# First stage of a hybrid decoder layer: deeper W_in and key buffers, forget logits and token scaling on ScalarE, diagonal maxima in one pass

## The chip, the core and the metric

The kernel runs on one core of a Trainium2 chip. Five engines take part, each with an instruction queue of its own that it works off strictly in order: TensorE (PE in the profile; its weight loads are PEld), VectorE (DVE), ScalarE (ACT), GpSimd (POOL) and SyncE (SP, which here only issues DMAs). An instruction that waits for another engine, or for a DMA, holds back everything behind it on its own engine.

The metric is the device time of one execution in microseconds (us), as the median of several. The kernel before took 2691.55 us (three runs, 2686.87 to 2695.32).

## The reference, cut to what matters

One decoder layer over 2048 tokens of width 1024, all in float32. The change lies in the part before the softmax:

```python
a = rms_norm(h, pre_mix_g)                      # per token: h * rsqrt(mean(h^2)) * g
z = a @ w_in                                    # 1024 -> 2568 columns
q, k, v, f, u_sg, v_sg = split(z)               # 512, 512, 512, 8, 512, 512
log_f = log_sigmoid(f + f_bias)                 # 8 heads
c = cumsum(log_f, over tokens)
logits = q k^T / 8 + c[t] - c[s]   (causal), softmax, times v
u = gelu(u_sg); v = layer_norm(gelu(v_sg), ln_g, ln_b)
y_sg = u * (tril(w_s) @ v + b_s)                # within chunks of 128 tokens
```

What follows (the projection, a feed-forward part and a gated embedding) is not touched.

## The kernel before

The first stage runs over four **blocks** of 512 tokens (`block`, `b` = 0 to 3). In each block TensorE multiplies the transposed, normalised tokens (`wide`, eight places of 128 input rows) with six **groups** of W_in columns (`GROUPS`): v_sg (344 columns), the rest of v_sg with a part of u (344), f with the rest of u (344), q, k and v (512 each). A group has four steps `n` (128 tokens each, or 128 columns for q and k); a step is 24 matmuls (8 rows of W_in by 3 products of high and low halves) into one of **two** PSUM places `pacc`, and ends with an evacuation in `dones`. A step can only begin when the evacuation of the step two before it is done. Steps are counted 0 to 23 through a block; the f and u group is steps 8 to 11, q is 12 to 15.

Each piece of W_in is loaded by SP to a raw place (`wraw`, L319), cast to its high half by ScalarE (L96) and subtracted to its low half by GpSimd (L100) into one of 12 places `wsp`.

Around the steps, `mine` and `hooks` place further work:

- `fu_done` (L357, L358): VectorE adds the forget bias to 8 columns (`zf`), then ScalarE takes the gelu of the others (`ug`). The two instructions read the same PSUM place.
- `layer_norm` of v (L110, L111, L413 to L417): root on GpSimd, then for each of 4 tiles two VectorE operations (gain, bias), a GpSimd copy and a VectorE subtraction (`vn`).
- `x_norm` of the next block's tokens (L290 to L296): squares on ScalarE, sum on VectorE, the root (`xr`, L111) on GpSimd, and the scaling of each 128x1024 tile on VectorE (L296).
- `log_sigmoid` (L376 to L393): a polynomial on 128x32 numbers, all on VectorE but for the sigmoid.
- `qk_done` and `put_v`: ScalarE writes the high half and VectorE the low half of a 128x512 tile to one of two places `stg`, which SP stores.
- `maxima(b)`, for the block before, spread between the matmuls by `Filler`: for each head q times 512 keys at a time into a place `pM`, and the row maximum on VectorE (L172; on the diagonal also L175 with the causal mask). Its keys and queries come in by DMAs that ScalarE issues (L159, L165), keys into two places `KM`.

Blocks 0 to 2 prepare the tokens of the next block, block 3 does not. Attention follows at about 560 us, with the last block's maxima spread in it, and the feed-forward part from about 1165 us on. The instructions are not issued in the order of the Python text: a list scheduler orders each engine's queue when the program is built.

Of the kernel before, what the change touches and what calls it, by code (L numbers as in the profile page):

```python
# [34 lines left out]
def trunk(ctx, tc, x, p, w_in, f_bias, sg_ln_g, sg_ln_b, sg_w, sg_b, att_out_g, sg_out_g,  # L35
# [36 lines left out]
    c0_all = const1.tile([P, NB, H], F32, name="c0_all")  # L72
    dmask_r = const1.tile([P, P], F32R, name="dmask")
# [4 lines left out]
    ident_r = const1.tile([P, P], F32R, name="ident_r")  # L78
    ve.tensor_copy(ident_r, ident)
# [54 lines left out]
    NKM = 2  # L134
# [4 lines left out]
    for t in QM:  # L139
        ve.memset(t[HD:HD + 2].bitcast(F32), 1.0)  # L140

    def maxima(b):

        def rows(h, mh):
            ps = place_m()
            pe.transpose(ps[:8, :P], mh.rearrange("p a b -> p (a b)").bitcast(F32), ident)
            mr = msm.tile([8, P], F32, name="mr", bufs=1)
            sc.copy(mr, ps[:8, :P])
            for l in range(2):
                sy.dma_start(qS[b, h, P + l].rearrange("(t i) -> t i", i=P), mr[4 * l:4 * l + 4])  # L150

        last = None
        ps = place_m()
        pe.matmul(ps[:, :H], ident[:, 0:1].broadcast_to([P, P]), c_all[:, 4 * b], start=True, stop=True)
        ve.tensor_copy(c0_all[:, b], ps[:, :H])
        n = 0
        for h in range(H):
            q = QM[h % 2]
            sc.dma_start(q[:HD].bitcast(F32), qS[b, h, :HD])  # L159
            mx = msm.tile([P, 4, 6], F32, name="mx")  # L160
            po.memset(mx, NEG)
            for c in range(b + 1):
                km = KM[n % NKM]
                n += 1
                sc.dma_start(km[:HD + 2].bitcast(F32), kS[c, h, HD:])  # L165
                for tt in range(4):
                    w = TB if c < b else P * (tt + 1)
                    ps = place_m()
                    pe.matmul(ps[:, :w], q[:, tt * P:(tt + 1) * P], km[:, :w], start=True, stop=True)  # L169
                    full = w if c < b else w - P  # L170
                    if full:
                        ve.tensor_reduce(mx[:, tt, c:c + 1], ps[:, :full], AX.X, ALU.max)  # L172
# [48 lines left out]
    with ExitStack() as ph:  # L221
        cst = pool(ph, "cst1", 1)
        stg = pool(ph, "stg", 2)
        small = pool(ph, "small1", 2)
        wrp = pool(ph, "wrp", 3)
# [16 lines left out]
        ones = cst.tile([P, P], F32, name="ones")  # L242
# [4 lines left out]
        def prep_consts():  # L247
# [6 lines left out]
            ve.memset(ones, 1.0)  # L254
            po.affine_select(out=upper, in_=ones, pattern=[[1, P]], compare_op=ALU.is_ge, fill=0.0,
# [23 lines left out]
        def x_norm(st, parts, rest=None):  # L279
            ss = st["ss"]  # L280
            for t0, t1 in parts:
# [13 lines left out]
                for tt in range(t0, t1):  # L295
                    ve.tensor_scalar(st["xs"][tt], st["xs"][tt], r[:, tt - t0:tt - t0 + 1], None, ALU.mult)  # L296
# [31 lines left out]
        def block(b, aT, hooks, fill, first=None):  # L328
# [18 lines left out]
            def uv_done(tt, ps):  # L347
# [4 lines left out]
                ve.tensor_scalar(gv[:, tt], gv[:, tt], mu[:, tt:tt + 1], None, ALU.add)  # L352
                junk = sg1.tile([P, 512], F32, name="junk")
                sc.activation(junk, gv[:, tt], AF.Square, accum_out=ss[:, tt:tt + 1])

            def fu_done(tt, ps):
                ve.tensor_tensor(zf[:, tt], ps[:, :H], fb, ALU.add)  # L357
                sc.activation(ug[:, tt, :336], ps[:, H:344], AF.Gelu_apprx_tanh)  # L358
# [15 lines left out]
            def log_sigmoid():  # L374

                ve.tensor_scalar(e, zf, -1.0, None, ALU.mult)  # L376
                ve.tensor_tensor(e, zf, e, ALU.min)
# [31 lines left out]
            def layer_norm():  # L409

                r = rstd_of(small, ss, 4, AW, "lnr")
                for tt in range(4):
                    ve.scalar_tensor_tensor(gv[:, tt], gv[:, tt], r[:, tt:tt + 1], lng, ALU.mult, ALU.mult)  # L413
                    ve.tensor_tensor(gv[:, tt], gv[:, tt], lnb, ALU.add)
# [1222 lines left out]
```

## Time and profile before

| | us |
|---|---|
| median of three runs | 2691.55 (2686.87 to 2695.32) |
| the profiled execution's own time | 2682.36 |
| its span, first to last instruction | 2680.6 |

| engine | busy us | share of the span |
|---|---|---|
| PEld (weight loads) | 2123.4 | 79% |
| VectorE | 1843.5 | 69% |
| ScalarE | 1341.6 | 50% |
| GpSimd | 806.6 | 30% |

Most of the profile's groups name what ended the idle time of an engine ("<-ACT ug L358" reads: the engine stood until the ScalarE instruction of line 358 that writes `ug`). Matmuls overlap in the array, so the times of single matmuls add up to more than the time that passes; idle time of PE is what counts.

### The profile page before, as it was taken

The page shows a single profiled execution, that of the slowest core. Times are in us where ns is not written, and L with a number is a line of the kernel's source. Part 1 is how long each engine was busy: PE and PEld are TensorE (multiplying, and loading weights), DVE is VectorE, ACT ScalarE, POOL GpSimd, SP SyncE. Part 2 cuts the span into 40 slices and gives each one's busy share as a digit, 9 for nine tenths or more (in the row PEclk, how much of TensorE's full clock was granted, in tenths as well). Part 3 has the DMA queues.
Part 4 walks back from the last instruction along what each step waited for, and adds up shares of the span by engine and source line. Part 5 has one row for each costly group of instructions (what it writes and reads, how often), then busy time and mean ns, then how long its engine had stood idle before and what let it go on. Part 6 is the DMA issues. An engine that isn't in the chain of part 4 may idle for free.

```text
span 2680.6 us, 37427 instructions
## 1 busy us (share of the span) xinstructions
PE 2610.0 (97%) x12316; PEld 2123.4 (79%) x12316; DVE 1843.5 (69%) x3214; ACT 1341.6 (50%) x2632; POOL 806.6 (30%) x695
## 2 busy tenths in 40 slices
PE   8999999999999999989999999999999999999999
PEld 7797978777677777767787788888888888888887
DVE  5547586866877655588888677677786596875443
ACT  6443433358877777655555455445435544453111
POOL 5444343410000100244434223236360171401211
PEclk9999999999999999999999999999999999999999
DMA  5565756588977876455665854447466644673331
GB/s 168 149 186 142 204 143 170 139 219 213 230 190 189 182 180 148 128 173 202 207 200 178 305 178 148 148 148 272 152 196 218 197 155 131 215 246 112 110 120 61
DMA packets 440083, 472.62 MB, mean 176 GB/s; under 512 B 155088, under 2 KB 269520, under 8 KB 439888
## 3 DMA queue, kind: packets, MB, share of 16 engines
q1 hardware_dynamic: 429651, 454.16, 57.5%
q10 hardware_dynamic: 10237, 16.07, 2.2%
q8 instruction: 97, 1.59, 0.3%
q14 instruction: 98, 0.80, 0.1%
HBM read 336.28 MB, written 133.82 MB: 175 GB/s over the span
## 4 chain that ended last, share of the span: by engine, by line
PE 53%; DVE 2%; DMA 1%; issue 0%; POOL 0%; ACT 0%; SPq 0%; DVEq 0%; ACTq 0%
PE pf L106 17%; PE pf L105 17%; PE pf L104 17%; DMA w1raw<-in_w_ff_dram 1%; PE pf L1485 1%; DVE w1p L999 0%; DMA B<-jS 0%; DVE ws L1183 0%; PE pf L1023 0%; DVE C L999 0%; DVE hq L1202 0%; PE pf L1478 0%; DVE z L750 0%; DVE v L1242 0%; DVE B L999 0%
## 5 line engine op out<-in xcount | busy, mean ns | idle before, releaser
L104 PE MATMUL pf<-B,w1p 128*128 128x512 f32 x752 | 298.4, 397 | 5.0 <-ACT w1p L996 3.9
L106 PE MATMUL pf<-B,w1p 128*128 128x512 f32 x752 | 296.7, 395 | 5.2 <-DVE w1p L999 5.1
L105 PE MATMUL pf<-B,w1p 128*128 128x512 f32 x752 | 297.3, 395 | 0.0
L1210 POOL TENSOR_TENSOR hq<-hq,hq 128x512 f32<-128x512 f32 x128 | 197.4, 1552 | 327.8 <-ACT hq L1204 292.1
L660 DVE TENSOR_TENSOR hl<-pr,hl 128x512 fp32r<-128x512 f32 (+1 forms) x320 | 193.0, 612 | 101.7 <-ACT hl L659 88.4
L100 POOL TENSOR_TENSOR wsp<-wraw,wsp 128x344 fp32r<-128x344 f32 (+1 forms) x176 | 199.5, 1150 | 190.0 <-ACT wsp L96 177.1
L651 ACT ACTIVATE pr<-pS,bias 128x512 f32<-128x512 f32 (+1 forms) x320 | 196.3, 622 | 101.2 <-PE pS L647 65.5
L172 DVE TENSOR_REDUCE mx<-pM 128x1 f32<-128x512 f32 (+3 forms) x288 | 169.8, 597 | 72.9 <-PE pM L169 72.0
L104 PE MATMUL pacc<-wsp,wide 128*128 128x344 f32 (+1 forms) x480 | 166.7, 347 | 9.9 <-ACT ug L358 6.8
L104 PE MATMUL pf<-R,L 128*128 128x512 f32 x452 | 176.1, 390 | 0.0
L105 PE MATMUL pf<-R,L 128*128 128x512 f32 x452 | 176.1, 390 | 0.0
L106 PE MATMUL pf<-R,L 128*128 128x512 f32 x452 | 176.0, 389 | 0.0
L106 PEld LDWEIGHTS pf<-B,w1p 128*128 128x128 f32 x752 | 142.0, 189 | 40.2 <-DVE w1p L999 7.8
L104 PEld LDWEIGHTS pf<-B,w1p 128*128 128x128 f32 x752 | 141.6, 188 | 39.5 <-ACT w1p L996 4.6
L105 PEld LDWEIGHTS pf<-B,w1p 128*128 128x128 f32 x752 | 141.8, 189 | 31.4
L106 PE MATMUL pacc<-wsp,wide 128*128 128x344 f32 (+1 forms) x480 | 162.6, 339 | 0.6 <-DVE wide L117 0.6
L105 PE MATMUL pacc<-wsp,wide 128*128 128x344 f32 (+1 forms) x480 | 162.4, 338 | 0.0
L659 ACT CAST hl<-pr 128x512 fp32r<-128x512 f32 (+3 forms) x272 | 146.4, 549 | 6.7 <-PE pO L674 0.8
L999 DVE TENSOR_TENSOR L<-lr,L 128x512 fp32r<-128x512 f32 x113 | 98.8, 874 | 70.2 <-ACT L L996 69.8
L996 ACT CAST L<-lr 128x512 fp32r<-128x512 f32 x113 | 70.2, 621 | 152.2 <-PE pf L105 117.5
L999 DVE TENSOR_TENSOR w1p<-ws,w1p 128x512 fp32r<-128x512 f32 (+1 forms) x136 | 120.6, 890 | 30.0 <-ACT w1p L996 28.0
L996 ACT CAST w1p<-w1raw 128x512 fp32r<-128x512 f32 (+1 forms) x123 | 73.3, 598 | 127.2 <-PE pf L105 124.5
(446 smaller groups left out, 7191.7 us busy)
## 6 DMA issues: line engine op xcount, KB each, us to landing
hidC<-hq SPq DMA_DIRECT2D x224, 256.0 KB
lr<-hidC SPq DMA_DIRECT2D x224, 256.0 KB
w1raw<-in_w_ff_dram SPq DMA_DIRECT2D x64, 512.0 KB
w1raw<-in_w_ff_dram SPq DMA_DIRECT2D x128, 256.0 KB
wraw<-in_w_in_dram SPq DMA_DIRECT2D x96, 256.0 KB
wraw<-in_w_in_dram SPq DMA_DIRECT2D x88, 172.0 KB
KM<-kS ACTq DMA_DIRECT2D x80, 132.0 KB
jS<-C SPq DMA_DIRECT2D x19, 512.0 KB
```

The costliest lines, as they stand in the source:

```text
L100: e.tensor_tensor(dst[:, 1], src, dst[:, 0].bitcast(F32), ALU.subtract)
L104: pe.matmul(ps, l[0], r[0], start=first, stop=False)
L105: pe.matmul(ps, l[0], r[1], start=False, stop=False)
L106: pe.matmul(ps, l[1], r[0], start=False, stop=last)
L172: ve.tensor_reduce(mx[:, tt, c:c + 1], ps[:, :full], AX.X, ALU.max)
L651: sc.activation(pr[:, off:], ps[:, off:], AF.Exp, bias=bias_of(b)[:, j, h:h + 1])
L659: sc.copy(hl[:, 0, off:], pr[:, off:])
L660: ve.tensor_tensor(hl[:, 1, off:], pr[:, off:], hl[:, 0, off:].bitcast(F32), ALU.subtract)
L996: sc.copy(dst[:, 0], src)
L999: (po if lo == "pool" else ve).tensor_tensor(dst[:, 1], src, dst[:, 0].bitcast(F32), ALU.subtract)
L1210: po.tensor_tensor(t, x, y, op)
L1485: pe.transpose(ps[:, kk], hts[t][g][:, kk * P:(kk + 1) * P], ident)
```

## The change

In the first stage:

- six raw W_in places (`wrp`) for three, three evacuation places (`stg`) for two;
- four key places `KM` for two, and key loads issued two pieces ahead, query loads one head ahead;
- `fu_done` copies the forget logits with ScalarE, and the bias is added for four tiles at once in `log_sigmoid`;
- the scaling of tokens is cut into halves of 512 columns that ScalarE does (for the first two tiles of the kernel VectorE does one half);
- the mean of v is no longer subtracted in a pass of its own: ScalarE's square takes it as a bias, and the gain and bias passes of `layer_norm` become two fused operations;
- the polynomial uses fused operations, 10 in place of 17;
- the diagonal's maximum is one fused operation over the whole width with a 128x512 mask `wmask`, in place of a reduction and a masked operation of 128;
- the matrix of ones is gone; the triangle's last column stands in for it.

```diff
@@
+    ident_r = const1.tile([P, P], F32R, name="ident_r")
+    ve.tensor_copy(ident_r, ident)
...
-    NKM = 2
+    NKM, LEAD = 4, 2
...
+    wmask = mst.tile([P, TB], F32, name="wmask")
+    ve.memset(wmask[:, :TB - P], 0.0)
+    ve.tensor_copy(wmask[:, TB - P:], dmask)
...
+        def load_k(i):
+            h, c = divmod(i, b + 1)
+            if h < H:
+                sc.dma_start(KM[i % NKM][:HD + 2].bitcast(F32), kS[c, h, HD:])
...
-            sc.dma_start(q[:HD].bitcast(F32), qS[b, h, :HD])
...
+                load_k(n + LEAD)
+                if c == b:
+                    load_q(h + 1)
                 n += 1
-                sc.dma_start(km[:HD + 2].bitcast(F32), kS[c, h, HD:])
...
-                    full = w if c < b else w - P
-                    if full:
-                        ve.tensor_reduce(mx[:, tt, c:c + 1], ps[:, :full], AX.X, ALU.max)
-                    if c == b:
-                        dg = ps[:, w - P:w]
-                        ve.tensor_tensor_reduce(out=dg, in0=dg, in1=dmask, scale=1.0, scalar=NEG,
-                                                op0=ALU.add, op1=ALU.max, accum_out=mx[:, tt, 5:6])
+                    if c < b:
+                        ve.tensor_reduce(mx[:, tt, c:c + 1], ps, AX.X, ALU.max)
+                    else:
+                        ve.tensor_tensor_reduce(out=ps[:, :w], in0=ps[:, :w], in1=wmask[:, TB - w:], scale=1.0, scalar=NEG,
+                                                op0=ALU.add, op1=ALU.max, accum_out=mx[:, tt, c:c + 1])
...
-        stg = pool(ph, "stg", 2)
+        stg = pool(ph, "stg", 3)
-        wrp = pool(ph, "wrp", 3)
+        wrp = pool(ph, "wrp", 6)
...
-                    ve.tensor_scalar(st["xs"][tt], st["xs"][tt], r[:, tt - t0:tt - t0 + 1], None, ALU.mult)
+                    for hf in range(2):
+                        xh, rt = st["xs"][tt][:, hf * 512:(hf + 1) * 512], r[:, tt - t0:tt - t0 + 1]
+                        if rest is not None and not hf:
+                            ve.tensor_scalar(xh, xh, rt, None, ALU.mult)
+                        else:
+                            sc.activation(xh, xh, AF.Copy, scale=rt)
...
-                ve.tensor_scalar(gv[:, tt], gv[:, tt], mu[:, tt:tt + 1], None, ALU.add)
                 junk = sg1.tile([P, 512], F32, name="junk")
-                sc.activation(junk, gv[:, tt], AF.Square, accum_out=ss[:, tt:tt + 1])
+                sc.activation(junk, gv[:, tt], AF.Square, bias=mu[:, tt:tt + 1], accum_out=ss[:, tt:tt + 1])
 
             def fu_done(tt, ps):
-                ve.tensor_tensor(zf[:, tt], ps[:, :H], fb, ALU.add)
+                sc.copy(zf[:, tt], ps[:, :H])
                 sc.activation(ug[:, tt, :336], ps[:, H:344], AF.Gelu_apprx_tanh)
...
-                ve.tensor_scalar(e, zf, -1.0, None, ALU.mult)
-                ve.tensor_tensor(e, zf, e, ALU.min)
+                ve.tensor_tensor(zf, zf, fb.unsqueeze(1).broadcast_to([P, 4, H]), ALU.add)
+                ve.scalar_tensor_tensor(e, zf, -1.0, zf, ALU.mult, ALU.min)
...
-                for k in (13, 11, 9, 7, 5, 3, 1):
-                    ve.tensor_tensor(pl, pl, s2, ALU.mult)
-                    ve.tensor_scalar(pl, pl, 1.0 / k, None, ALU.add)
-                ve.scalar_tensor_tensor(pl, pl, -2.0, s_, ALU.mult, ALU.mult)
+                ve.tensor_scalar(pl, s2, 1.0 / 17, None, ALU.mult)
+                for k in (15, 13, 11, 9, 7, 5, 3):
+                    ve.scalar_tensor_tensor(pl, pl, 1.0 / k, s2, ALU.add, ALU.mult)
+                ve.scalar_tensor_tensor(pl, pl, 1.0, s_, ALU.add, ALU.mult)
...
-                    ve.scalar_tensor_tensor(gv[:, tt], gv[:, tt], r[:, tt:tt + 1], lng, ALU.mult, ALU.mult)
-                    ve.tensor_tensor(gv[:, tt], gv[:, tt], lnb, ALU.add)
+                    ve.scalar_tensor_tensor(gv[:, tt], gv[:, tt], mu[:, tt:tt + 1], lng, ALU.add, ALU.mult)
+                    ve.scalar_tensor_tensor(gv[:, tt], gv[:, tt], r[:, tt:tt + 1], lnb, ALU.mult, ALU.add)
```

The scheduler orders the queues anew. The first place is **ScalarE in block 0, around the gelus of steps 8 to 10** (`zf` forget logits, `ug` gelu, `xss` the squares of the next block's tokens, `xt<-xt,xr` their scaling, `wsp` casts of W_in). Before:

```order
L290 ACTIVATE junk,xss<-xt 128x512
L358 ACTIVATE ug<-pacc 128x336
L96 CAST wsp<-wraw 128x512
L290 ACTIVATE junk,xss<-xt 128x512 x4
L358 ACTIVATE ug<-pacc 128x336
L290 ACTIVATE junk,xss<-xt 128x512 x2
L96 CAST wsp<-wraw 128x512
L358 ACTIVATE ug<-pacc 128x336
```

and of the change (L376 is the copy of the logits, L377 the gelu, L305 the squares, L316 the scaling):

```order
L305 ACTIVATE junk,xss<-xt 128x512 x2
L376 COPY zf<-pacc 128x8
L377 ACTIVATE ug<-pacc 128x336
L305 ACTIVATE junk,xss<-xt 128x512 x5
L376 COPY zf<-pacc 128x8
L377 ACTIVATE ug<-pacc 128x336
L316 ACTIVATE xt<-xt,xr 128x512 x6
L376 COPY zf<-pacc 128x8
L377 ACTIVATE ug<-pacc 128x336
```

Six scalings of the next block's tokens now stand ahead of the third copy and gelu (step 10). In blocks 1 and 2 three stand there.

The second place is **VectorE in block 0 from the root of the layer norm on** (`lnr` the root's argument, `gv` the gelu of v, `vn` its halves, `xss` and `xr` the tokens' sums and the root's argument). Before:

```order
L110 TENSOR_SCALAR lnr<-lnss 128x4
L413 SCALAR_TENSOR_TENSOR gv<-gv,lnr,lng 128x512 x2
L357 TENSOR_TENSOR zf<-pacc,fb 128x8
L414 TENSOR_TENSOR gv<-gv,lnb 128x512 x2
L413 SCALAR_TENSOR_TENSOR gv<-gv,lnr,lng 128x512
L417 TENSOR_TENSOR vn<-gv,vn 128x512 x2
L414 TENSOR_TENSOR gv<-gv,lnb 128x512
L357 TENSOR_TENSOR zf<-pacc,fb 128x8
L413 SCALAR_TENSOR_TENSOR gv<-gv,lnr,lng 128x512
L417 TENSOR_TENSOR vn<-gv,vn 128x512
L414 TENSOR_TENSOR gv<-gv,lnb 128x512
L293 TENSOR_TENSOR xss<-xss 128x1 x3
```

and of the change:

```order
L110 TENSOR_SCALAR lnr<-lnss 128x4
L431 SCALAR_TENSOR_TENSOR gv<-gv,mu,lng 128x512
L432 SCALAR_TENSOR_TENSOR gv<-gv,lnr,lnb 128x512 x2
L435 TENSOR_TENSOR vn<-gv,vn 128x512
L432 SCALAR_TENSOR_TENSOR gv<-gv,lnr,lnb 128x512
L435 TENSOR_TENSOR vn<-gv,vn 128x512
L432 SCALAR_TENSOR_TENSOR gv<-gv,lnr,lnb 128x512
L435 TENSOR_TENSOR vn<-gv,vn 128x512
L308 TENSOR_TENSOR xss<-xss 128x1
L435 TENSOR_TENSOR vn<-gv,vn 128x512
L110 TENSOR_SCALAR xr<-xss 128x1
L308 TENSOR_TENSOR xss<-xss 128x1 x2
```

The forget logits are gone from this queue, and after the root each tile needs one operation on `gv` in place of two; the first root argument of the tokens (`xr`) stands behind all four subtractions.

The third place is **GpSimd in block 0 behind the root of the layer norm** (`lnr`). Before:

```order
L111 TENSOR_TENSOR lnr<-lnr,mhalf 128x4
L100 TENSOR_TENSOR wsp<-wraw,wsp 128x512 x2
L415 TENSOR_SCALAR vn<-gv 128x512 x2
L100 TENSOR_TENSOR wsp<-wraw,wsp 128x512
L415 TENSOR_SCALAR vn<-gv 128x512 x2
L111 TENSOR_TENSOR xr<-xr,mhalf 128x1 x2
```

and of the change:

```order
L111 TENSOR_TENSOR lnr<-lnr,mhalf 128x4
L100 TENSOR_TENSOR wsp<-wraw,wsp 128x512
L433 TENSOR_SCALAR vn<-gv 128x512 x4
L111 TENSOR_TENSOR xr<-xr,mhalf 128x1 x3
L100 TENSOR_TENSOR wsp<-wraw,wsp 128x512 x4
L111 TENSOR_TENSOR xr<-xr,mhalf 128x1
```

Three roots now follow each other, and the fourth stands behind four subtractions of W_in.

More of the change, by code (lines that the diff above doesn't have):

```diff
@@ L77, in trunk @@
                      base=0, channel_multiplier=1)
-    ident_r = const1.tile([P, P], F32R, name="ident_r")
-    ve.tensor_copy(ident_r, ident)
     def bcast(pool, name, v, n):
@@ L156, in maxima, with load_q @@
         n = 0
+        def load_k(i):
+            h, c = divmod(i, b + 1)
+            if h < H:
+                sc.dma_start(KM[i % NKM][:HD + 2].bitcast(F32), kS[c, h, HD:])
+        def load_q(h):
+            if h < H:
+                sc.dma_start(QM[h % 2][:HD].bitcast(F32), qS[b, h, :HD])
+        load_q(0)
+        for i in range(LEAD):
+            load_k(i)
         for h in range(H):
             q = QM[h % 2]
-            sc.dma_start(q[:HD].bitcast(F32), qS[b, h, :HD])
-            mx = msm.tile([P, 4, 6], F32, name="mx")
+            mx = msm.tile([P, 4, NB], F32, name="mx")
             po.memset(mx, NEG)
@@ L241, in trunk @@
         sgb = cst.tile([P, H], F32, name="sgb")
-        ones = cst.tile([P, P], F32, name="ones")
         upper = cst.tile([P, P], F32, name="upper")
@@ L253, in prep_consts @@
             ve.memset(csum[:, 0], 0.0)
-            ve.memset(ones, 1.0)
-            po.affine_select(out=upper, in_=ones, pattern=[[1, P]], compare_op=ALU.is_ge, fill=0.0,
+            ve.memset(upper, 1.0)
+            po.affine_select(out=upper, in_=upper, pattern=[[1, P]], compare_op=ALU.is_ge, fill=0.0,
                              base=0, channel_multiplier=-1)
@@ L382, in log_sigmoid @@
                 ve.tensor_tensor(s2, s_, s_, ALU.mult)
-                ve.tensor_scalar(pl, s2, 1.0 / 17, 1.0 / 15, ALU.mult, ALU.add)
-                for k in (13, 11, 9, 7, 5, 3, 1):
-                    ve.tensor_tensor(pl, pl, s2, ALU.mult)
-                    ve.tensor_scalar(pl, pl, 1.0 / k, None, ALU.add)
-                ve.scalar_tensor_tensor(pl, pl, -2.0, s_, ALU.mult, ALU.mult)
+                ve.tensor_scalar(pl, s2, 1.0 / 17, None, ALU.mult)
+                for k in (15, 13, 11, 9, 7, 5, 3):
+                    ve.scalar_tensor_tensor(pl, pl, 1.0 / k, s2, ALU.add, ALU.mult)
+                ve.scalar_tensor_tensor(pl, pl, 1.0, s_, ALU.add, ALU.mult)
                 ve.tensor_scalar(zf, zf, 0.0, None, ALU.min)
-                ve.tensor_tensor(pl, pl, zf, ALU.add)
+                ve.scalar_tensor_tensor(pl, pl, -2.0, zf, ALU.mult, ALU.add)
                 ve.tensor_copy(car[:, 0], csum[:, b])
@@ L397, in run_sum @@
                 pe.matmul(ps[:, :32], upper, pl.rearrange("p a h -> p (a h)"), start=True, stop=False)
-                pe.matmul(ps[:, :32], ones, car[:, 0:4].rearrange("p a h -> p (a h)"), start=False, stop=True)
+                pe.matmul(ps[:, :32], upper[:, P - 1:P].broadcast_to([P, P]), car[:, 0:4].rearrange("p a h -> p (a h)"), start=False, stop=True)
                 ve.tensor_copy(c_all[:, 4 * b:4 * b + 4].rearrange("p a h -> p (a h)"), ps[:, :32])
```

## The prediction

> **What bounds the kernel now.** I began with the table of stretches, one row for each part of the first stage in which TensorE stood, then the waits of TensorE over these stretches (25 to 560 us).
>
> ```profile
> core 0: us, PE busy (x) PEld busy (x) DVE busy (x) ACT busy (x) POOL busy (x), PEclk, DMA share, GB/s
> 0.00:25.00 25.00, 17.86 (x72) 14.01 (x72) 17.27 (x47) 17.25 (x45) 12.76 (x23) 0.80 0.79 223
> 25.00:74.00 49.00, 43.26 (x274) 42.10 (x272) 26.11 (x56) 28.41 (x82) 25.92 (x27) 0.99 0.41 123
> ...
> 178.00:240.00 62.00, 55.58 (x281) 47.74 (x280) 47.25 (x138) 28.00 (x73) 33.78 (x35) 0.94 0.48 128
> ...
> 330.00:370.00 40.00, 33.77 (x168) 27.04 (x167) 38.15 (x94) 17.75 (x43) 23.34 (x24) 1.00 0.47 127
> ...
> 460.00:560.00 100.00, 92.49 (x478) 77.70 (x477) 80.63 (x216) 36.85 (x85) 47.08 (x51) 1.00 0.54 152
> ```
>
> The stage is TensorE's: the change leaves its matmuls as they are, so only its idle time can go. Length less PE busy gives 5.74 us in block 0's stretch, 6.42 in block 1's, 6.23 in block 2's (where VectorE is busy 38.15 of 40 us) and 7.51 in block 3's. What it waited for (us in total, times, longest):
>
> ```profile
> PE pacc L104 <- ACT ug L358: 9.0, 5, 2.5
> PE pM L169 <- DVE mx L172: 4.8, 8, 1.3
> PE pacc L104 <- DVE stg L117: 4.3, 3, 1.9
> PE tp L440 <- DVE gv L435: 2.7, 2, 1.6
> PE pacc L106 <- POOL wsp L100: 1.5, 3, 0.9
> PE pmx L104 <- DVE gv L427: 1.3, 1, 1.3
> ```
>
> The first row names ScalarE's gelu. The tile `zf` tells whom ScalarE itself waited for (its columns are shortest, median and longest ns; then us and times of a wait):
>
> ```profile
> L357 DVE TENSOR_TENSOR zf<-pacc,fb x16: 150/152/156, 60.8 to 498.4; 128x8 f32<-128x8 f32 x16
> L377 DVE TENSOR_TENSOR lse<-zf,lse x4: 179/1262/1279, 77.9 to 502.3; 128x32 f32<-128x32 f32 x4
> ...
>   ACT ug L358: 34.3, 14
> ```
>
> VectorE's addition of 0.15 us held the gelu 34.3 us in 14 cases, since it is queued behind the layer norm. So the first row's five waits are VectorE's queue too, as the next three rows are by name. Three stretches of slower clock follow on such waits:
>
> ```profile
> 73.40:77.00 3.60, 3.60 (x9) 2.84 (x10) 2.90 (x7) 1.11 (x3) 3.38 (x4) 0.53 0.20 67
> ...
> 203.00:206.70 3.70, 3.70 (x14) 3.54 (x15) 3.69 (x12) 1.97 (x6) 1.04 (x2) 0.54 0.26 72
> ...
> 216.70:220.20 3.50, 3.05 (x7) 2.48 (x8) 3.33 (x9) 1.56 (x5) 2.60 (x3) 0.51 0.28 75
> ```
>
> At a clock near 0.53, each costs 3.6 x 0.47 = 1.7 us, 5.1 in all. The Trainium skill, "TensorE: Matmul & The Clock Gate", Part 1, has the half clock come after an idle window of about 3.4 us; here it came though no wait exceeded 2.5 us, so the trace speaks against that length. By the rule the shortening of such waits would return no clock, and my sum would be 1.7 us less.
>
> **Block 0.** The timeline of TensorE, with the wait in brackets:
>
> ```profile
> 61.46 0.43 PE L104 MATMUL pacc<-wsp,wide 128*128 128x344 f32 x1 [2.01 <-ACT ug L358]
> 67.07 0.43 PE L104 MATMUL pacc<-wsp,wide 128*128 128x344 f32 x1 [1.56 <-ACT ug L358]
> 73.29 0.69 PE L104 MATMUL pacc<-wide,wsp 128*128 128x512 f32 x1 [2.17 <-ACT ug L358]
> 88.11 0.50 PE L104 MATMUL pacc<-wide,wsp 128*128 128x512 f32 x1 [1.78 <-DVE stg L117]
> ```
>
> The first two waits go: the copy and the gelu need only ScalarE, with squares ahead of them. The third has a new cause: six token scalings stand ahead of the third gelu, and they need roots behind the whole layer norm. Durations for that chain:
>
> ```profile
> L413 DVE SCALAR_TENSOR_TENSOR gv<-gv,lnr,lng 128x512 f32<-128x512 f32 x16 | 21.0, 1315 | 4.5 <-POOL lnr L111 4.5
> ...
> L417 DVE TENSOR_TENSOR vn<-gv,vn 128x512 fp32r<-128x512 f32 x16 | 16.4, 1027 | 1.6 <-POOL vn L415 1.6
> ...
> L414 DVE TENSOR_TENSOR gv<-gv,lnb 128x512 f32<-128x512 f32 x16 | 13.2, 829 | 0.0
> ```
>
> ```profile
> L290 ACT ACTIVATE junk<-xt 128x512 f32<-128x512 f32 x24 | 15.1, 631 | 0.4
> ...
> L358 ACT ACTIVATE ug<-pacc 128x336 f32<-128x336 f32 x16 | 7.2, 451 | 37.5 <-DVE zf L357 34.3 <-PE pacc L106 3.2
> ...
> L148 ACT COPY mr<-pM 8x128 f32<-8x128 f32 x22 | 5.4, 246 | 19.0 <-PE pM L146 19.0
> ```
>
> ```profile
> L111 POOL TENSOR_TENSOR xr<-xr,mhalf 128x1 f32<-128x1 f32 x12 | 8.3, 697 | 5.7 <-DVE xr L110 3.9 <-DVE xss L293 0.9 <-PE pM L169 0.8
> ```
>
> ```profile
> 56.34 1.02 POOL L111 TENSOR_TENSOR lnr<-lnr,mhalf 128x4 f32<-128x4 f32 x1
> ```
>
> From the root's end at 57.36: four fused operations at 1.315 and four subtractions at 1.027 are 9.37 (the fourth mean-and-gain pass runs while the root is computed), 0.3 for the tiny sums: 67.0. One root of 0.697, then six scalings at the squares' 0.631 (the copy form isn't in the trace; a square is the same tile): 71.5; copy 0.246 and gelu 0.451: 72.2. TensorE wants this place at 73.29 less 2.17, 2.01 and 1.56, that is 67.55: a wait of 4.7. The lower end takes all eight at L414's 0.829, the cheapest two-input row of this size: 6.63, and a wait of 1.9. I take **3.5**, nearer the upper end, whose rows are of the same operations. The fourth wait, 1.78 us for the low half of q behind the polynomial, goes: seven of its 17 operations go, and the token scalings on VectorE ahead of them. So block 0 gains 5.74 + 1.78 - 3.5 = **4.0 us**.
>
> **Blocks 1 and 2** have the same chain, with three scalings in front and with maxima between:
>
> ```profile
> 191.79 1.02 POOL L111 TENSOR_TENSOR lnr<-lnr,mhalf 128x4 f32<-128x4 f32 x1
> ...
> 334.36 1.01 POOL L111 TENSOR_TENSOR lnr<-lnr,mhalf 128x4 f32<-128x4 f32 x1 [1.26 <-DVE lnr L110]
> ```
>
> ```profile
> L172 DVE TENSOR_REDUCE mx<-pM 128x1 f32<-128x512 f32 (+3 forms) x288 | 169.8, 597 | 72.9 <-PE pM L169 72.0
> ```
>
> ```profile
> 202.89 0.46 PE L104 MATMUL pacc<-wsp,wide 128*128 128x344 f32 x1 [2.52 <-ACT ug L358]
> ...
> 208.54 0.39 PE L104 MATMUL pacc<-wide,wsp 128*128 128x512 f32 x1
> ...
> 338.55 0.33 PE L169 MATMUL pM<-KM,QM 128*128 128x128 f32 x1 [0.82 <-DVE mx L172]
> ...
> 342.75 0.45 PE L169 MATMUL pM<-KM,QM 128*128 128x384 f32 x1 [1.34 <-DVE mx L172]
> ...
> 349.36 0.40 PE L104 MATMUL pacc<-wide,wsp 128*128 128x512 f32 x1
> ```
>
> Block 1: the root ends at 192.81; 9.4 of layer norm, 1.8 for three maxima at 0.597 or less, 0.4 of sums, one root (0.7), three scalings (1.9), copy and gelu (0.7): 207.7. It is wanted at 208.54 - 2.52 - 1.7 of clock = 204.3: a wait of up to 3.4, and 0.7 with L414's 0.829. I take **2.5**, and leave 0.9 for small waits on W_in: 6.42 - 3.4 + 1.7 for one of its two slow stretches = **4.7 us**. Block 2: the root ends at 335.37; four fused operations and three subtractions (8.3), six maxima (3.6), sums (0.3); then one subtraction and one maximum (1.6) ahead of the second root's argument, that root (0.7), the third scaling (0.6), copy and gelu (0.7): 351.2. It is wanted at 349.36 - 0.82 - 1.34 = 347.2: a wait of up to 4.0, and 1.3 with the shorter operations. I take **3.0**: 6.23 - 3.0 = **3.2 us**.
>
> **Block 3** scales no tokens. Its waits for the scaling of `gv` (L435, 2.7) stay as they are in the code; half of L427's 1.3 I leave too; those for maxima and polynomial go. 7.51 - 3.3 = **4.2 us**.
>
> **Costed at nothing.** Three more raw places and the new `stg`: W_in's lows kept TensorE 1.5 us in the whole stage, which I gave back above. Key loads ahead are hidden by matmuls now and later; ScalarE, on which they queue, is busy 28 to 58% in these stretches. The diagonal's one pass trades a fixed cost for none, beside matmuls. At the start VectorE gets three more fillings ahead of the first tokens:
>
> ```profile
> 1.13 1.03 DVE L138 MEMSET KM<- 128x512 f32 x2
> ```
>
> That is about 1.4 us later; half-width scaling returns some 0.9 of it. I take -0.5, between -1.5 and +2 (7.14 us are idle there and evacuations now stand ahead of squares). Attention: 0, from -1 to +1.
>
> **The sum:** 4.0 + 4.7 + 3.2 + 4.2 - 0.5 = 15.6, say 16 us. The profiled execution took 2682.36 (span 2680.6), so 2666.4 for one like it; the median of the runs shown is 9.2 us higher, 2691.55, and I forecast from it: **2675.5 us**.
>
> **Rivals.**
>
> 1. *The scaling wait stays small.* If the roots come early, the three waits (9.0) and the other two slow stretches (3.4) go as well: 16 + 12.4 = 28 us, 2663. The ceiling, all idle time of the four stretches (25.9), the 1.78 and the 5.1 of clock, is 33 us: 2659. For it: ScalarE had slack in each stretch. Against: the queue rows, three to six scalings ahead of a gelu.
> 2. *VectorE's chain is not shortened.* The `lse` row above shows one operation at 0.18 and at 1.26 us: where it meets a GpSimd subtraction it waits. The new chain has as many exposed operations as the old. Then the waits are 4.7, 3.4 and 4.0, 3.1 more than I took, the `stg` waits (4.3) stay, and so does the clock's 1.7: 16 - 9.1 = 7 us gained, 2684.5. The Trainium skill, "SBUF — State Buffer", Who interferes with whom, says that a VectorE instruction with two SBUF inputs contends with a GpSimd instruction that reads SBUF, the loser waiting for the whole instruction; the fused operations all have two, and the `lse` row agrees.
> 3. *Slower: ScalarE's queue is the new bound.* On GpSimd the tokens' roots compete with W_in's subtractions:
>
> ```profile
> L100 POOL TENSOR_TENSOR wsp<-wraw,wsp 128x344 fp32r<-128x344 f32 (+1 forms) x176 | 199.5, 1150 | 190.0 <-ACT wsp L96 177.1
> ```
>
> If the scaling ahead of the third gelu had to wait for a root behind four of them (4.6), with the root and the scaling (1.3) the wait before q grows from 4.7 to 10.6 us, in three blocks 32 against the 9 assumed: 2691.55 - 16 + 23 = 2698.5. It turns the sign from about 8 us per block on (25 in all). Against: only the fourth root stands behind four subtractions in block 0's rows.
> 4. *The change doesn't do what it says:* a deeper buffer that SP fills no earlier. It is not in the sum, so it would change nothing.
>
> **How the numbers follow.** Forecast (gain 8 to 26 us) 0.57; rival 1 0.13; rival 2, and any case that ends within 8 us of before, 0.23; rival 3 0.07. 0.3% is 8 us, about what a measurement of this kernel can tell from no change. Faster is 0.57 + 0.13 = 0.70, same 0.23, slower 0.07. The range runs from the ceiling, 2659, to 2691, no gain: beyond it lie rival 3 and the worse half of rival 2, under 2 in 10.
>
> **What would show it.** Right: no wait of a `pacc` matmul for the gelu in the first two cases of each block; the wait for `ug` before the first q step named by ScalarE scalings and 2 to 5 us long; no `stg` wait behind the polynomial; slow stretches of the clock two or fewer in blocks 0 and 1. Wrong: waits at the first q step of 8 us or more, or new waits for W_in's low halves, since GpSimd now does roots and copies in a row.

## The result, and the profile after

The changed kernel took 2670.56 us (median of 7, 2667.26 to 2682.38) against 2687.77 us for the kernel before (7 runs, 2685.51 to 2695.32) on the same chip: a ratio of 0.9933, 95% interval 0.9913 to 0.9953, or 18 us faster by the ratio (13 to 23), 17 by the medians.

The two profiled executions don't show it: both have a span of 2680.6 us. The changed kernel's was the slowest of its seven; the other's, at 2682.36, was faster than all seven of its own. So each was profiled once more. What came out is read best from one row per execution: the stretch from the start to the first matmul of attention (its end is the start of the first `pS` matmul). Columns: the stretch in us, its length, busy time (and count) of PE, PEld, DVE, ACT and POOL, the clock, and DMA share and GB/s. Before, in two executions:

```profile
0.00:564.76 564.76, 529.94 (x2763) 455.63 (x2763) 360.18 (x925) 244.43 (x570) 252.60 (x272) 0.98 0.60 165
```

```profile
0.00:570.80 570.80, 535.71 (x2763) 460.06 (x2763) 361.82 (x925) 244.66 (x570) 252.26 (x272) 0.97 0.59 164
```

After, in two executions:

```profile
0.00:553.30 553.30, 525.38 (x2761) 455.67 (x2761) 325.09 (x784) 263.63 (x617) 245.71 (x272) 0.98 0.61 169
```

```profile
0.00:549.42 549.42, 524.13 (x2760) 454.39 (x2761) 328.44 (x787) 263.85 (x617) 246.03 (x272) 0.99 0.61 170
```

The first stage ends at 567.8 us before and 551.4 after, as means of two: 16.4 us. Attention, first to last `pS` matmul, took 547.8 and 555.1 us before, 558.9 and 550.9 after, so it moves by 7 to 8 us from one execution to the next of either kernel; behind it lie 1566 to 1568 us in all four. The gain is the first stage's, and the profiled execution of after lost it again in attention by chance.

Length less PE busy is idle time; but PE busy itself fell too, for the same matmuls. The clock records of the trace say why in part: TensorE runs at 0.50 in stretches of 3.4 us, and half of the time that it was busy in them is lost. Split in three, as means of the two executions:

| first stage, us | before | after | gain |
|---|---|---|---|
| TensorE idle | 35.0 | 26.6 | 8.4 |
| lost to the half clock | 11.9 | 7.8 | 4.1 |
| the rest: busy at full clock | 520.9 | 516.9 | 4.0 |

The first 25 us alone hold 1.1 of the 8.4 and 2.4 of the 4.1. The rest has no name in the profile: nearly the same matmuls took a little longer without a wait being shown, some 2.3 us of it those of the maxima, and the cause stays open.

The stretches that the prediction used, in the profile after (same columns):

```profile
0.00:25.00 25.00, 18.71 (x91) 15.53 (x91) 17.32 (x55) 20.05 (x53) 9.65 (x21) 0.93 0.84 247
25.00:74.00 49.00, 44.31 (x264) 42.65 (x264) 21.52 (x45) 32.57 (x93) 30.83 (x32) 0.93 0.46 133
...
178.00:240.00 62.00, 57.59 (x298) 49.54 (x297) 39.67 (x104) 33.87 (x79) 36.68 (x37) 0.97 0.54 151
...
330.00:370.00 40.00, 36.70 (x171) 30.29 (x172) 31.37 (x81) 19.24 (x41) 19.10 (x21) 0.96 0.47 131
...
460.00:560.00 100.00, 92.33 (x459) 76.05 (x458) 76.31 (x175) 38.00 (x84) 43.77 (x48) 0.98 0.57 160
```

What TensorE waited for between 25 and 560 us, in the same profile (us in total, times, longest):

```profile
PE pacc L104 <- ACT ug L377: 6.7, 2, 4.7
PE pacc L104 <- DVE stg L117: 6.2, 3, 2.4
PE pM L187 <- DVE mx L189: 4.4, 6, 1.2
PE pmx L415 <- DVE gv L445: 2.3, 1, 2.3
```

The gelu's row has two waits left of five, and TensorE's timeline puts both at the first q step of a block; the two below are at its third q step, for a low half of q:

```profile
68.60 0.79 PE L104 MATMUL pacc<-wide,wsp 128*128 128x512 f32 x1 [4.68 <-ACT ug L377]
84.22 0.50 PE L104 MATMUL pacc<-wide,wsp 128*128 128x512 f32 x1 [2.07 <-DVE stg L117]
```

```profile
200.86 0.50 PE L104 MATMUL pacc<-wide,wsp 128*128 128x512 f32 x1 [2.03 <-ACT ug L377]
215.50 0.50 PE L104 MATMUL pacc<-wide,wsp 128*128 128x512 f32 x1 [2.38 <-DVE stg L117]
```

ScalarE's timeline shows what stands behind the first of them:

```profile
57.28 0.45 ACT L377 ACTIVATE ug<-pacc 128x336 f32<-128x336 f32 x1
64.37 3.78 ACT L316 ACTIVATE xt<-xt,xr 128x512 f32<-128x512 f32 x6 [6.64 <-POOL xr L111]
68.06 0.14 ACT L376 COPY zf<-pacc 128x8 f32<-128x8 f32 x1
68.11 0.44 ACT L377 ACTIVATE ug<-pacc 128x336 f32<-128x336 f32 x1
68.45 2.17 ACT L96 CAST wsp<-wraw 128x512 fp32r<-128x512 f32 x4
```

ScalarE stands 6.64 us for the root of the next block's tokens, then does six scalings, and only then the gelu that TensorE needs. Four casts of W_in come out in a row behind it: they too had stood in the queue.

### The profile page after: what moved, and what is told of

The parts are those of the page before. It is cut to its first block, busy times and chain, and to the rows that moved or that the text cites. A ratio compares the mean times of both kernels' runs of the same rounds, so it can differ in the third digit from the quotient of the medians.

```text
span 2680.6 us, 37229 instructions
## 1 busy us (share of the span) xinstructions
PE 2610.9 (97%) x12316; PEld 2124.6 (79%) x12316; DVE 1799.1 (67%) x3048; ACT 1361.4 (51%) x2678; POOL 798.4 (30%) x695
## 4 chain that ended last, share of the span: by engine, by line
PE 48%; DMA 1%; DVE 1%; POOL 1%; issue 0%; ACT 0%; DVEq 0%; POOLq 0%; ACTq 0%
PE pf L106 16%; PE pf L105 16%; PE pf L104 16%; DMA w1raw<-in_w_ff_dram 1%; PE pf L1503 1%; POOL hq L1228 0%; DVE w1p L1017 0%; DVE ws L1201 0%; DMA B<-jS 0%; DVE hq L1220 0%; PE pf L1496 0%; DVE v L1260 0%; ACT hq L1221 0%; PE pf L1041 0%; POOL tmp L1093 0%
## 5 line engine op out<-in xcount | busy, mean ns | idle before, releaser
L100 POOL TENSOR_TENSOR wsp<-wraw,wsp 128x344 fp32r<-128x344 f32 (+1 forms) x176 | 192.9, 1131 | 119.6 <-ACT wsp L96 116.8
L189 DVE TENSOR_REDUCE mx<-pM 128x1 f32<-128x512 f32 x192 | 129.7, 685 | 43.2 <-PE pM L187 42.2
```

What stands on the lines that cost most here:

```text
L100: e.tensor_tensor(dst[:, 1], src, dst[:, 0].bitcast(F32), ALU.subtract)
L189: ve.tensor_reduce(mx[:, tt, c:c + 1], ps, AX.X, ALU.max)
```

## The experiments

Ratios are to the kernel before on the same chip, with 95% intervals. First the two kernels again, each profiled once more.

**change_again** (no edit)

> The changed kernel once more, for a second trace of it: its profiled execution was the longest of its seven runs (2682.38 us against a median of 2670.56), and in it attention began 11.5 us earlier than before and ended at the same time. Theory 1 (the loss in attention is chance of that execution, from transfers that landed late): the first stage again ends near 553 us, attention from its first score to its last takes 545 to 552 us as before (547.8), the span is near 2669. Theory 2 (what starts earlier is always given back in attention): attention takes about 559 us again and the span stays near 2680. Ratio to before 0.991 to 0.996.

2671.16 us, 0.9929 (0.9908 to 0.9950). Its stage ended at 549.4 and its span was 2667.1 us: the gain is real, and in the first stage.

**before_again** (no edit; one execution)

> The kernel before once more, for a second trace: the first stage ends near 564 us and attention takes about 548 us if the first trace was an ordinary one; a span 5 us longer (2685, as the timed runs) would show where executions of the same kernel differ.

2693.86 us; the stage ended at 570.8 and attention took 555.1 us. Two profiles of one kernel differ by 6 us in the stage and 7 in attention: a difference of one trace below that says nothing.

**logits_alone**: the copy of the logits, put into the kernel before.

```diff
-                ve.tensor_tensor(zf[:, tt], ps[:, :H], fb, ALU.add)
+                sc.copy(zf[:, tt], ps[:, :H])
...
+                ve.tensor_tensor(zf, zf, fb.unsqueeze(1).broadcast_to([P, 4, H]), ALU.add)
```

> The kernel before with one part of the change: the forget logits are copied by ScalarE and the bias is added for four tiles at once. Theory 1 (five waits for the gelu are VectorE's queue, 9.0 us, with up to 5.1 us of slow clock behind them): all waits of pacc for the gelu of the ug tile are gone, 7 to 14 us faster than before, ratio 0.995 to 0.997. Rival (the waits move to the next step, since VectorE's queue stays as long as it was): under 4 us gained, and the waits for stg behind the polynomial grow by as much.

2692.23 us, 1.0001 (0.9990 to 1.0013): a miss. TensorE's waits between 25 and 560 us:

```profile
PE pacc L106 <- POOL wsp L100: 9.3, 6, 4.6
PE pM L169 <- DVE mx L172: 5.7, 6, 2.4
PE pacc L104 <- DVE stg L117: 4.7, 2, 3.0
```

The gelu's 9.0 us are gone, to the last wait. In their place stand 9.3 us for W_in's low halves, which had been 1.5: TensorE reached the first q step at 66.41 us instead of 73.29, and waited there for W_in instead. The rival was right about the gain; it had named the waits for `stg`, which hardly grew (4.7 us for 4.3).

**scale_on_vectore**: the change, with the later blocks' token scalings on VectorE.

```diff
+                    if rest is None:
+                        ve.tensor_scalar(st["xs"][tt], st["xs"][tt], r[:, tt - t0:tt - t0 + 1], None, ALU.mult)
+                        continue
...
-                        if rest is not None and not hf:
+                        if not hf:
```

> The change with one part undone: blocks 1 to 3's tokens are scaled by VectorE again, a 128x1024 tile at a time (the first four tiles' halves as in the change except tiles 2 and 3). Theory 1 (the 4.7 and 2.0 us waits ahead of the first q step in blocks 0 and 1 are the scalings on ScalarE): these waits are gone, and the waits for stg behind the polynomial grow, by 1 to 3 us each in blocks 0 to 2; net -4 to +4 us against the change. Rival (the waits there come from other work on ScalarE): the 4.7 us wait stays.

2676.81 us, 0.9941 (0.9923 to 0.9959), not told apart from the change. The wait for the gelu before q is gone, so the scalings in ScalarE's queue did make it; low halves of W_in (3.9 us) and maxima (6.3 for 4.4) took its place, and not the waits for `stg`, which had been expected to grow:

```profile
PE pM L187 <- DVE mx L189: 6.3, 8, 1.6
PE pacc L104 <- DVE stg L117: 6.1, 2, 4.0
PE pacc L106 <- POOL wsp L100: 3.9, 5, 1.5
```

**raws_undone**: the change, with three raw places.

```diff
-        wrp = pool(ph, "wrp", 6)
+        wrp = pool(ph, "wrp", 3)
```

> The change, with three raw W_in places instead of six; nothing else is different. Theory A (new, from logits_alone, where W_in's low halves held TensorE 9.3 us): the raw places are what uncovers the other edits. ScalarE's casts wait for W_in loads some 50 times for 60 to 75 us in all (48 times and 63.3 us in the kernel before, 9 times and 8.8 us in the change); TensorE waits 5 to 10 us for low halves of W_in between 25 and 560 us, and more than half of the gain goes: 2681 to 2690 us, 0.996 to 1.000 of the kernel before. Theory B (of the prediction): raw places are worth nothing: 2671 us, 0.993, low-half waits under 1.5 us.

2683.38 us, 0.9974 (0.9960 to 0.9988), which lies clear of the change's interval: three places cost 11 to 12 us (0.0041 to 0.0045 of 2690) by the middle values, over half of the gain; with the intervals it is some 5 to 18 us. The scheduler orders ScalarE's queue anew for three places, so this is the price of the places with the order that they bring. The size was theory A's; its mechanism was not, since the low halves held TensorE 0.6 us. The stage:

```profile
0.00:560.08 560.08, 529.93 (x2761) 458.20 (x2761) 326.56 (x786) 262.21 (x617) 249.62 (x272) 0.98 0.61 167
```

It is 8.7 us longer than the change's mean: 3.5 more idle, 4.0 more lost to the clock (11.85 for 7.8), 1.2 in the rest. Casts waited for loads as forecast (the tile `wraw`, who waited for it: us and times):

```profile
  ACT wsp L96: 80.3, 54
```

and such a wait holds the whole queue. ScalarE and TensorE at 34 us:

```profile
34.31 0.48 ACT L96 CAST wsp<-wraw 128x344 fp32r<-128x344 f32 x1 [1.63 <-DMA wraw<-in_w_in_dram]
34.70 0.36 ACT L116 ACTIVATE wide<-tp,g_pre 128x128 fp32r<-128x128 f32 x1
```

```profile
35.11 0.47 PE L104 MATMUL pacc<-wsp,wide 128*128 128x344 f32 x1 [1.97 <-ACT wide L116]
```

The tokens' evacuation stood behind a cast that stood for a load, and TensorE waited 1.97 us for it. Block 0's first q step came at 74.17 us, for 68.60 and 68.24 in the change, so most of the loss was made by then. Its wait for the gelu there was 5.28 us, for 4.68. These are two places shown; the other waits are small and spread.

**logits_raws** and **raws_alone**: the kernel before with six raw places, with and without the copy of the logits.

```diff
-        wrp = pool(ph, "wrp", 3)
+        wrp = pool(ph, "wrp", 6)
```

> The kernel before with two edits: ScalarE's copy of the forget logits (as in logits_alone) and six raw W_in places. Theory A: the 9.3 us that logits_alone waited for low halves fall under 2, no gelu wait returns, and the time is 7 to 12 us below before: 2680 to 2685, 0.9955 to 0.9975. Theory B: raw places change nothing, so as logits_alone: 2692, 1.000, low-half waits of 5 us or more (GpSimd's own queue sets them, not the loads).

2687.40 us, 0.9985 (0.9974 to 0.9995): 1 to 7 us faster, less than theory A's range. The low halves fell from 9.3 to 5.9 us, not under 2.

> The kernel before with six raw W_in places and nothing else. Theory A: the copy of the logits is worth nothing in any company (alone 1.0001; taken out of the change, 0.9913 against 0.9929), so the gain of logits_raws is that of the raw places, and this run gives as much: 2686 to 2689, 0.9975 to 0.999; casts wait for loads under 35 us in all, against 63.3. Theory B: the two need each other, since in the kernel before TensorE waited only 1.5 us for low halves of W_in: no gain, 2691 to 2693, 0.9995 to 1.0005, with the gelu's waits of before (9.0 us) still there.

2687.35 us, 0.9991 (0.9980 to 1.0001): between the two theories, and not told apart from either. Casts waited 11.1 us for loads, the low halves 0.7, and the gelu's waits stood at 9.1 as before. So the raw places are worth some 5 us at most in the kernel before and 11 to 12 in the change. That a late load holds more where scalings, copies and casts share a queue would explain it; no run separates this from the new order of the queues.

**scale_late**: the change, with the later blocks' scalings put behind the gelu of step 11 in ScalarE's queue. TensorE's order is that of the change.

```diff
+        last_gelu = []
...
+                        elif rest is None and last_gelu:
+                            with tc.issue_after(last_gelu[-1].ins):
+                                sc.activation(xh, xh, AF.Copy, scale=rt)
...
-                sc.activation(ug[:, tt, :336], ps[:, H:344], AF.Gelu_apprx_tanh)
+                last_gelu.append(sc.activation(ug[:, tt, :336], ps[:, H:344], AF.Gelu_apprx_tanh))
```

> The change, with ScalarE's token scalings of the later blocks issued behind the last gelu of the gate (the row of step 11) instead of ahead of the third. Theory A: they are what holds the gelu ahead of the first q step (4.7 us in block 0, 2.0 in block 1): both waits fall under 0.5, one or two stretches of slow clock go, and since the work moved is due later, 3 to 6 us are gained: 2665 to 2668, 0.991. Rival: the wait moves, as it did where the scalings stood on VectorE, to the scaled evacuation of q and to low halves: 2671 to 2677, 0.993 to 0.995.

2659.07 us, 0.9876 (0.9863 to 0.9889): faster than both kernels, 12 us under the change by medians (2670.56 and 2671.16) and 14 to 15 by the ratios, at least twice what theory A gave. The stage:

```profile
0.00:532.00 532.00, 518.23 (x2760) 450.04 (x2761) 322.62 (x784) 264.00 (x617) 245.72 (x272) 1.00 0.63 175
```

It is 19.4 us shorter than the change's mean: 12.8 of idle time, all 7.8 of the half clock, 1.3 more in the rest. Of the 7.8, 1.6 us lie in the first 25 us, ahead of all that the edit moves. The gain grows from block to block: the first q steps came 5.5, 11.3, 14.4 and 17.2 us earlier than in the change. Attention took 557.8 us in this execution, within its spread. ScalarE, around the same gelus as above:

```profile
59.41 0.46 ACT L382 ACTIVATE ug<-pacc 128x336 f32<-128x336 f32 x1
59.86 3.23 ACT L96 CAST wsp<-wraw 128x512 fp32r<-128x512 f32 x6
63.12 0.17 ACT L381 COPY zf<-pacc 128x8 f32<-128x8 f32 x1
63.18 0.46 ACT L382 ACTIVATE ug<-pacc 128x336 f32<-128x336 f32 x1
63.52 0.72 ACT L319 ACTIVATE xt<-xt,xr 128x512 f32<-128x512 f32 x1
```

No wait for a root ahead of the gelus, the casts done between two of them, and the scalings behind. The first q step came at 62.92 us. TensorE's waits, 25 to 560 us:

```profile
PE pM L187 <- DVE mx L189: 4.4, 6, 1.2
...
PE pmx L420 <- DVE gv L450: 1.3, 1, 1.3
...
PE pacc L104 <- DVE stg L117: 0.3, 1, 0.3
PE pacc L106 <- POOL wsp L100: 0.3, 1, 0.3
```

The gelu's wait went without an heir, and the wait for q's low half went with it (0.3 us for 6.2). Why, VectorE's and ScalarE's timelines in the profile after show (L117 writes the low half, L116 the high half that it is computed from):

```profile
71.27 0.40 DVE L308 TENSOR_TENSOR xss<-xss 128x1 f32<-128x1 f32 x1 [5.32 <-ACT junk L305]
...
76.99 0.18 DVE L398 TENSOR_SCALAR lss<-lse 128x32 f32<-128x32 f32 x1 [2.58 <-ACT lse L397]
...
78.26 4.65 DVE L404 SCALAR_TENSOR_TENSOR lpl<-lpl,lss 128x32 f32<-128x32 f32 x7
...
83.48 0.68 DVE L117 SCALAR_TENSOR_TENSOR stg<-pacc,stg 128x512 fp32r<-128x512 f32 x1
```

```profile
79.03 0.59 ACT L116 ACTIVATE stg<-pacc 128x512 fp32r<-128x512 f32 x1
```

The high half was done at 79.62. The low half stood in VectorE's queue behind the polynomial, and the polynomial was late because VectorE had stood 5.32 us for ScalarE's squares and 2.58 for its sigmoid, which stand behind the scalings. In scale_late the polynomial's last operation ended at 73.37 us, for 83.36, while the first q step came only 5.7 us earlier.

**old_passes**, **norm_undone**, **stg_keys_undone** and **logits_undone**: the change with one part taken back each. They are the polynomial in 17 operations and the diagonal in two passes; the layer norm in five passes; two evacuation places, two key places and no key ahead; the forget bias added on VectorE for every tile.

```diff
-                for k in (15, 13, 11, 9, 7, 5, 3):
-                    ve.scalar_tensor_tensor(pl, pl, 1.0 / k, s2, ALU.add, ALU.mult)
+                for k in (13, 11, 9, 7, 5, 3, 1):
+                    ve.tensor_tensor(pl, pl, s2, ALU.mult)
+                    ve.tensor_scalar(pl, pl, 1.0 / k, None, ALU.add)
...
-                    if c < b:
-                        ve.tensor_reduce(mx[:, tt, c:c + 1], ps, AX.X, ALU.max)
+                    full = w if c < b else w - P
+                    if full:
+                        ve.tensor_reduce(mx[:, tt, c:c + 1], ps[:, :full], AX.X, ALU.max)
...
-                sc.activation(junk, gv[:, tt], AF.Square, bias=mu[:, tt:tt + 1], accum_out=ss[:, tt:tt + 1])
+                ve.tensor_scalar(gv[:, tt], gv[:, tt], mu[:, tt:tt + 1], None, ALU.add)
+                sc.activation(junk, gv[:, tt], AF.Square, accum_out=ss[:, tt:tt + 1])
...
-    NKM, LEAD = 4, 2
+    NKM, LEAD = 2, 0
...
-        stg = pool(ph, "stg", 3)
+        stg = pool(ph, "stg", 2)
...
-                sc.copy(zf[:, tt], ps[:, :H])
+                ve.tensor_tensor(zf[:, tt], ps[:, :H], fb, ALU.add)
```

> The change, with the polynomial of the log-sigmoid in 17 operations and the diagonal maxima in two passes, as before. Theory A: beside matmuls both are hidden but for what VectorE's queue holds: waits of TensorE for maxima rise from 4.4 us by 0.5 to 2, for the evacuation of q from 5.3 by 1 to 2: 2 to 4 us slower, 2673 to 2676, 0.994 to 0.995. Rival (VectorE's chain is the bound): 8 us or more slower, 2679 or over, 0.996 or over. Of the prediction, which costed the one pass at nothing and let the wait for the evacuation go with the shorter polynomial: 2674 to 2675.

> The change, with the layer norm of the gate in the five VectorE passes of before (the mean subtracted ahead of the square, then scale and gain, then bias) instead of two fused passes and a bias inside the square. VectorE has 13 to 15 us more to do in the stage, three quarters of it between the third projection and the first q step of each block. Theory A (VectorE's chain ahead of the roots decides): the wait for ug before q grows by about 0.6 to 2 us in each of three blocks, and the waits for evacuations by as much: 4 to 8 us slower than the change, 2675 to 2679, 0.994 to 0.996. Rival (ScalarE's scalings and not VectorE's passes set that wait): within 2 us of the change, 2669 to 2673, 0.992 to 0.9935.

> The change, with two evacuation places instead of three, and two key places with each key loaded when its maxima begin instead of two steps ahead; the six raw places stay. Theory A: of the buffers only the raw places count: within 3 us of the change, 2669 to 2674, 0.9915 to 0.9945, with waits of TensorE named DMA KM under 1 us. Rival: the buffers count together, and with the key loads late the maxima start late: waits at the maxima rise from 4.4 to over 8 us and the time is 5 us or more above the change, 2676 or over.

> The change, with the forget logits added on VectorE for every tile again instead of copied by ScalarE. Theory A (the edits cover each other: a removed wait counts only where the next supply is ready, which it is here): TensorE's waits for the gelu's row come back in the first three steps of the gate, with 6 to 9 us of waits for ug more than the 6.7 of the change, less what the later wait before q absorbs: 4 to 9 us slower than the change, 2675 to 2680, 0.994 to 0.997. Rival, from logits_alone, which gained nothing: the copy is worth nothing here too, 2671, 0.993.

| taken back | us | ratio | 95% interval |
|---|---|---|---|
| old_passes | 2674.53 | 0.9937 | 0.9925 to 0.9948 |
| norm_undone | 2677.17 | 0.9935 | 0.9922 to 0.9948 |
| stg_keys_undone | 2675.68 | 0.9929 | 0.9913 to 0.9944 |
| logits_undone | 2671.47 | 0.9913 | 0.9898 to 0.9928 |

None is told apart from the change (0.9908 to 0.9953): by the middle of its ratio each of these parts is worth 5 us or less, either way, against expectations of 2 to 4 (old_passes), 4 to 8 (norm_undone), nothing (stg_keys_undone) and 4 to 9 (logits_undone). TensorE's waits move little too: with the longer polynomial those for maxima stay at 4.4 us and those for `stg` are 6.7, for 6.2 and 5.3 in the change; with the longer layer norm the gelu's, expected to grow, fall to 3.7 us, for 6.7. The last is the instructive one. TensorE's timeline:

```profile
57.74 0.66 PE L104 MATMUL pacc<-wsp,wide 128*128 128x344 f32 x1 [2.19 <-ACT ug L377]
63.54 0.42 PE L104 MATMUL pacc<-wsp,wide 128*128 128x344 f32 x1 [0.30 <-ACT ug L377]
```

A wait behind VectorE is back, 2.19 us, but the first q step comes at 67.42 us, for 68.60 and 68.24 with the copy. There it had no wait at all. In the change it was ready at 63.92 us (68.60 less 4.68) and stood until about the same time, since the gelu came behind scalings that needed the tokens' root: a TensorE that arrives earlier only waits longer there.

The profiled executions side by side (one each, so the 6 us above hold), in us:

| kernel | stage ends | idle | half clock | rest |
|---|---|---|---|---|
| before, twice | 564.8, 570.8 | 34.8, 35.1 | 9.0, 14.8 | 521.0, 520.9 |
| logits_alone | 570.1 | 38.3 | 10.9 | 521.0 |
| raws_alone | 563.5 | 30.1 | 15.6 | 517.8 |
| logits_raws | 567.4 | 35.0 | 14.1 | 518.2 |
| raws_undone | 560.1 | 30.2 | 11.9 | 518.1 |
| after, twice | 553.3, 549.4 | 27.9, 25.3 | 8.9, 6.8 | 516.5, 517.3 |
| scale_on_vectore | 550.7 | 27.6 | 4.9 | 518.3 |
| scale_late | 532.0 | 13.8 | 0 | 518.2 |

## Why the prediction was right, and where it was not

**The bound was right.** The stage is TensorE's, the gain is its waits in the first stage, and attention gave and took nothing that can be told from its spread. The sum, 16 us, met 16.4 in the stage and 17 in the time. Its terms met less well, so that it met so closely is luck.

**The idle time was over-sized.** For the four blocks the prediction took 14.4 us of idle time and 1.7 of clock, and it lost 0.5 at the start. The runs gave 7.3 us of idle time and 1.6 of clock there, 3.5 at the start, and 4.0 of matmul time that it had no term for. Two errors cancelled: 7 us too much in the blocks, 8 from where it looked for none.

**Block 0's first two waits** went, as predicted. That they are worth their length was the step that failed: taken out alone (logits_alone) or put back alone (logits_undone) they are worth nothing that can be told from the noise, because the next thing TensorE needs, W_in's low halves in the one and the scaled tokens' root in the other, was no earlier.

**The new wait before q** was the right mechanism. It was taken as 3.5, 2.5 and 3.0 us; it measured 4.7, 2.0 and none. The upper end in block 0 was 4.7. The row of operations behind it came out shorter (8.1 us from the layer norm's root, 55.47, to the tokens' first root argument, 63.56, for 9.37 and 0.3), but TensorE came earlier as well (63.92 for 67.55), so the upper end was met by two shifts that cancelled.

**"The fourth wait, 1.78 us for the low half of q behind the polynomial, goes"** was wrong: it stayed at 2.07 us (2.38 in block 1). Its place, behind VectorE's polynomial, was right. But seven operations fewer hardly shortened that: in block 0 the ten took 5.3 us (78.05 to 83.36), the 17 before 5.6 (82.61 to 88.83 less an evacuation of 0.6 among them). And the polynomial began late, behind ScalarE's queue; scale_late, which leaves VectorE's operations as they are, took the wait away.

**"Costed at nothing"** failed for the raw places. The cover named was that W_in's low halves kept TensorE only 1.5 us. But the loads kept ScalarE 63.3 us in the kernel before:

```profile
  ACT wsp L96: 63.3, 48
```

In the change, where ScalarE carries more that TensorE needs, such waits cost 11 to 12 us, by raws_undone. So over half of the gain hangs on the edit that the sum put at nothing, while no other part, taken back alone, can be told from nothing. For the evacuation and key places nothing showed (0.9929, as the change).

**The start** was put at -0.5 us. Between 0 and 25 us idle time fell from 7.14 to 6.29 and the clock rose from 0.80 to 0.93. As means of both pairs of profiles, idle time fell by 1.1 us and the loss to the half clock from 4.0 to 1.6: 3.5 us gained, above the upper end of 2. Which edit did it is not shown.

**Block 3** was put at 4.2. From its first q step to the end of the stage it took 66.7 us before and 65.4 after in the two profiled executions (69.9 and 65.0 in the other two): 1.3 to 4.9, so this term is neither shown nor refuted.

**Rival 3** had the mechanism that matters most. ScalarE's queue did become the bound before q, at the low price of 4.7 us and not at 10.6, so the sign held. The reason that the rival gave, roots behind W_in's subtractions on GpSimd, did not show: in block 0 GpSimd stood 0.87 and 1.17 us for VectorE ahead of the roots. scale_late shows that this queue kept 12 us of what the change could give.

## What to carry to other kernels

A wait is worth its length only if what comes behind it is ready earlier: ask at every wait that goes what TensorE needs next, and which queue supplies it. When work moves to an engine with strict order, look at what it waits for, not only at how long it takes: here scalings of 0.63 us each cost 12 us because a root was late, and one placement behind the last urgent instruction gave them back. And split a stage into idle time, clock and the rest before crediting an edit, with two profiles of the same kernel to see what chance does.

## What the runs showed of the hardware

**The half clock comes in steps, and after short waits.** In the first stage of all these traces the slow stretches last 3.4 us or a multiple, at 0.50. One in the profile after, behind the wait of 2.38 us that ended at 215.50 (the 3.4 us before it, and in it):

```profile
213.10:216.51 3.41, 1.03 (x5) 0.86 (x5) 3.20 (x10) 0.68 (x2) 1.04 (x1) 1.00 0.15 52
216.51:219.92 3.41, 3.41 (x9) 2.64 (x8) 1.66 (x7) 0.00 (x0) 0.11 (x1) 0.50 0.92 253
```

TensorE was busy 1.03 of 3.41 us, and then ran 3.4 us at half rate. The 14 traces together, cut between 25 and 540 us into steps of 3.41 us that begin where the clock changed, show how short a wait is enough: of the steps at full clock, all 38 in which TensorE was busy for less than 0.45 of the time were followed by the half clock, 9 of 24 with 0.45 to 0.55, and none of 1994 with more.

The Trainium skill, "TensorE: Matmul & The Clock Gate", Part 1, has the gate work in windows of about 3.4 us that run freely, at half or full rate: length and rate agree. Its table of states puts the half rate behind an idle window; here a window that was a third busy was enough, and the measurement decides. In scale_late, where no such step was busy for less than 0.64, there was no half clock in the stage at all, so the clock pays again for what a wait costs: after the first 25 us, 6.3 us beside 12.5 of idle time.

**VectorE's operations with two inputs took longer beside GpSimd's.** The layer norm's passes, 1.315 us (gain), 0.829 (bias) and 1.027 (subtraction) before, are 0.833, 1.003 and 0.825 in the profile after:

```profile
L431 DVE SCALAR_TENSOR_TENSOR gv<-gv,mu,lng 128x512 f32<-128x512 f32 x16 | 13.3, 833 | 4.3 <-ACT junk L373 4.2
L432 DVE SCALAR_TENSOR_TENSOR gv<-gv,lnr,lnb 128x512 f32<-128x512 f32 x16 | 16.0, 1003 | 4.3 <-POOL lnr L111 4.3
L435 DVE TENSOR_TENSOR vn<-gv,vn 128x512 fp32r<-128x512 f32 x16 | 13.2, 825 | 1.9 <-POOL vn L433 1.6
```

The subtraction is the same code as before, and in logits_raws, whose layer norm is the old one, it took 0.811. So what changed is when it runs against other work, and such a row is no price of an operation by itself. That other work is GpSimd's: in both profiles each of these operations with no GpSimd instruction beside it took 0.67 to 0.75 us, and all longer ones, up to 1.8 us, overlapped one (15 of 16 gains and 10 of 16 subtractions before; 7 of 16 of L432 and 8 of 16 of L435 after). No run changed GpSimd's work alone.
